# Sigmoid of twelve gate tiles taken where they are computed, two y tiles kept on chip, and 35 small transfers begun by ScalarE

## The chip, the cores and the metric

The kernel runs on one core of a Trainium2 chip. The metric is device time in microseconds, from the first to the last instruction of one execution with what lies around it. A core has five engines that run side by side, each with its own instruction queue, worked through in order: TensorE (PE in the profile, with its weight loads as PEld), VectorE (DVE), ScalarE (ACT), GpSimd (POOL) and SyncE (SP). A DMA is begun by an instruction in one of these queues; before the change all are begun from SP's.

## The reference

One layer of a hybrid trunk on 1024 rows of 1024 channels, float32. One projection yields queries, keys and values for two branches of eight heads, and the two gates:

```python
h = x @ w_in[l]
qa, ka, va, qb, kb, vb, ga, gb = jnp.split(h, split_pts, axis=-1)
y_a = chunk_band_attention(...qa, ka, va, rel_bias[l]) @ w_proj_a[l]   # softmax over a band
y_b = stick_breaking_attention(...qb, kb, vb) @ w_proj_b[l]            # sigmoids, cumulative products
gate_a = jax.nn.sigmoid(ga + b_gate[l, :D])
gate_b = jax.nn.sigmoid(gb + b_gate[l, D:])
mix = (gate_a * y_a + gate_b * y_b) @ w_out[l]
x = layer_norm(DEEPNORM_ALPHA * x + mix, ln1_g[l], ln1_b[l])
...                                                                   # SwiGLU block, second layer norm
```

## The kernel before

Each large product is made from numbers split into a high and a low part (`split`: ScalarE casts the high part, VectorE or GpSimd subtracts), so three matmuls stand for one. Tiles of 128 partitions by 1024 columns come from pools of slots by tag (`SLOTS`): a new tile takes the slot of the one allocated so many allocations before with the same tag, and waits until that one is done with. The order of the instructions on each engine is set at build time from the order in which the program states them, with an estimate of what is ready when; at run time each engine keeps that order.

**First stage, the projections** (to about 367 us). 18 pairs of column blocks. One is computed plainly, the others with seven half-size products in place of eight (`pair_steps`, L176; matmuls at L173). The last six pairs are gates: pair j gives 128 channels of branch A's gate and the same 128 of branch B's, for j below `N_GATE` = 6. The halves of a result tile are put together by ScalarE's copies (L190, L199, L203, and L372 for the last one) and VectorE's additions (L186). `out_g` (L365) then stores the raw gate tile to `g_dr` from SP's queue. The tiles of this stage live in the slots in which the attention's queries, keys and values arrive later (tags qs, kh, kl, v), so the first of those loads wait for the last stores.

**Attention** (367 to about 676 us). Branch A's eight heads come first, then branch B's. A head has 12 value steps: a step transposes weights on TensorE (L575), splits them (`pt`, L111 and L112) and multiplies with the values (L588, L589). Scores for later steps run ahead (L478, L479). In branch A VectorE adds the bias (L509), ScalarE takes exponentials (L514) and GpSimd scales (L517). In branch B ScalarE takes two sigmoids (`kp` L542, `w` L543), VectorE a cumulative product (L546, L550), and GpSimd a product (L552). At the end of each half of a head ScalarE copies the 128-row result out of its bank (L603), and a transfer on chip of 64 rows by 512 columns (L604, 128 KB) brings the second half of the products to the partitions of the first. Three steps later GpSimd adds them into the pair's tile `yt` (L607). After the last of four additions `yt` is stored to `y_dr[i]` (L609). That is done for pairs 0 to 6; pair 7 is cut where it lies. There are 31 such small transfers, 16 of them in branch A.

**Fill.** Between the value steps TensorE is given other matmuls (`fill_all`, L616): first the remaining four gate tiles (pairs 6 and 7 of each branch, `gate`, L422, stored at L437), then branch A's output projection over eight channel blocks c (matmuls L675). For it `fetch_y` (L620) loads `y_dr[i]` back into `yraw`, and `cut_y` (L624) splits it into yh (ScalarE, L627) and yl (GpSimd, L628). For each c, `fetch_g` loads the gate tile gA, `sigma` (L699) takes its sigmoid in place on ScalarE (L701), queued half a block ahead, and VectorE multiplies the projection with it (L678). Blocks 0 to 4 are stored to `m_dr`, 5 to 7 are kept. The fill runs at 8 matmuls a head in branch A and at 40 in branch B.

**Merge** (676 to about 715 us). For c in the order 6, 7, 5, 4, 0, 1, 2, 3 the gate gB of branch B is loaded (L793), its sigmoid taken (L794), the projection of branch B multiplied with it (L805), branch A's part added (L806), and the sum split for the output projection. After that come the output projection, the layer norm and the SwiGLU block, which the change does not touch.

Of the kernel before, what the change touches and what calls it, by code (L numbers as in the profile page):

```python
# [49 lines left out]
def hybrid_trunk_kernel(ctx: ExitStack, tc, x, xt, w_in, b_gate, rel_bias, w_proj,  # L50
# [14 lines left out]
    def slot(tag, name, dtype=F32):  # L65
        return pool.tile([P, 1024], dtype, tag=tag, name=name, bufs=SLOTS[tag])
# [236 lines left out]
    def project_plain(i):  # L303
# [20 lines left out]
                store_hl(d[pair], h, t)  # L324
        return take

    def project(i):
        kind, pair = work[i][:2]
        tl = {}

        def tile_of(side):
            if side not in tl:
                tl[side] = cycle(QKV, f"c{side}_{i}")
            return tl[side]

        def c(name):
            return tile_of(name[1])[:, (LO, HI)[int(name[0]) - 1]]

        def out_qk(side):
            scale = (-0.125 if pair < 4 else 0.125) if side == "1" else 1.0  # L340
            t = tl[side]
            h = cycle(QKV, f"hi{side}_{i}", F32R)
            nc.scalar.activation(h, t, AF.Copy, scale=scale)
            nc.vector.scalar_tensor_tensor(t, t, scale, h.bitcast(F32), ALU.mult, ALU.subtract)
            d = (q_dr, k_dr)[side == "2"]
            store_hl(d[pair], h, t)

        def out_v(side):
            pr = pair + int(side) - 1
            vs = [cycle(QKV, f"v{pr}_{h}", F32R).rearrange("p (t c) -> p t c", t=8)  # L350
                  for h in range(2)]
            for hf in range(2):
                tp = bank("tr", f"vtp{pr}_{hf}")
                for j in range(4):
                    o = hf * HW + j * P
                    tr(tp[:, j * P:(j + 1) * P], tl[side][:, o:o + P], ident)
                t3 = tp.rearrange("p (t c) -> p t c", t=4)
                ts_ = slice(4 * hf, 4 * hf + 4)
                for h in range(2):
                    split(vs[h][:, ts_, 0:DH], vs[h][:, ts_, DH:P],  # L360
                          t3[:, :, h * DH:(h + 1) * DH])
            for h in range(2):
                dma(v_dr[2 * pr + h].rearrange("p (t c) -> p t c", t=8), vs[h].bitcast(F32))

        def out_g(side):  # L365
            dma(g_dr[2 * pair + int(side) - 1], tl[side])

        out = dict(qk=out_qk, v=out_v, g=out_g)[kind]

        def done(name, acc):  # L370
            if name == "21":
                nc.scalar.copy(c("21"), acc)  # L372
                out("1")
            elif name == "12":
                out("2")

        return pair_steps(f"p{i}", Wa[i], ops_x, c, done)
# [44 lines left out]
    def gate(i, w, half=lambda: None, then=lambda k: None):  # L422
        gt = slot("gt", f"gate{i}")
        for hf, cs in enumerate((LO, HI)):
            acc = bank("mm", f"gps{i}_{hf}")
            for k in range(KT):
                ks = slice(k * P, (k + 1) * P)
                for j, (lw, rx) in enumerate(((w[0], xh), (w[0], xl), (w[1], xh))):
                    mm(acc, lw[:, ks], rx[k][:, cs], start=(k == j == 0),  # L429
                       stop=(k == KT - 1 and j == 2))  # L430
                    yield 1.0
                if hf == 1:
                    then(k)
            nc.scalar.copy(gt[:, cs], acc)
            if hf == 0:
                half()
        dma(g_dr[i], gt)  # L437

    left(2)
    take = project_plain(0)  # L440
# [115 lines left out]
    def value_steps(hd, g, wt):  # L556

        br, h = hd["br"], hd["h"]
        reach = (4, 8)[br]
        q0 = 4 * g  # L560
        nm = f"{'ab'[br]}{hd['n']}_{g}"
        pv = []

        kbs = [4, 5, 6, 7, 3, 2, 1, 0] if g == 0 else [7, 6, 5, 4]
        steps = []
        for i, kb in enumerate(kbs):
            lo_q = max(q0, kb - reach)
            hi_q = min(q0 + 3, kb)
            n = (hi_q - lo_q + 1) * P
            pts = []  # L570

            def turn(kb=kb, lo_q=lo_q, hi_q=hi_q, n=n, pts=pts):
                tp = bank("tr", f"tp_{nm}_{kb}")
                for qb in range(lo_q, hi_q + 1):
                    tr(tp[:, (qb - lo_q) * P:(qb - lo_q + 1) * P],  # L575
                       wt[qb - q0][:, (kb - qb) * P:(kb - qb + 1) * P], ident)
                pt = slot("pt", f"pt_{nm}_{kb}", F32R)
                split(pt[:, 0:n], pt[:, HW:HW + n], tp[:, 0:n])
                pts.append(pt)

            def mult(i=i, kb=kb, lo_q=lo_q, n=n, pts=pts):
                v = hd["v"]
                if i == 0:
                    pv.append(bank("pv", f"pv_{nm}"))
                last = i == len(kbs) - 1
                cs = slice((lo_q - q0) * P, (lo_q - q0) * P + n)
                pt = pts[0]
                mm(pv[0][:, cs], v[:, kb, :], pt[:, 0:n], start=(i == 0), stop=False)  # L588
                mm(pv[0][:, cs], v[:, kb, :], pt[:, HW:HW + n], start=False, stop=last)  # L589
                if last:  # L590
                    yt = hd["yt"]()
                    r = slice(h * DH, (h + 1) * DH)
                    gs = slice(g * HW, (g + 1) * HW)
                    if hd["i"] == 7 and h == g == 1:
                        nc.scalar.copy(yt[r, gs], pv[0][DH:P])
                        nc.vector.tensor_tensor(yt[r, gs], pv[0][0:DH], yt[r, gs], ALU.add)
                    else:

                        if g == 0:
                            hd["yv"] = slot("yt", f"yv_{nm}")  # L600
                        yv = hd["yv"]
                        both, other = (yt, yv) if h == 0 else (yv, yt)
                        nc.scalar.copy(both[:, gs], pv[0])  # L603
                        dma(other[r, gs], both[(DH, 0)[h]:(P, DH)[h], gs])  # L604

                        def add():
                            nc.gpsimd.tensor_tensor(yt[r, gs], yt[r, gs], yv[r, gs], ALU.add)  # L607
                            if h == 1 and g == 1:
                                dma(y_dr[hd["i"]], yt)  # L609
                        later.append([3, add])  # L610

            steps.append((turn, mult))
        return steps


    def fill_all():  # L616
# [5 lines left out]
            dma(yraw[i], y_dr[i])  # L622

        def cut_y(i):  # L624
            yh[i] = slot("xt", f"yh{i}", F32R)
            yl[i] = slot("xt", f"yl{i}", F32R)
            nc.scalar.copy(yh[i], yraw[i])  # L627
            nc.gpsimd.tensor_tensor(yl[i], yraw[i], yh[i].bitcast(F32), ALU.subtract)  # L628

        def fetch_g(c):  # L630
            gA[c] = slot("gt", f"gA{c}")
# [17 lines left out]
        for i in range(first_gate, 16):  # L649
# [3 lines left out]
            else:  # L653
# [1 line left out]
                fetch_y(0)  # L655
                fetch_y(1)
                yield from gate(i, w[-1], lambda: half_of(i), then)
        sigma(gA[0], 0, 0)
        for cc in range(4):
            wh, wl = w[-1]  # L660
            if cc < 3:
                nxt = fetch_proj(0, cc + 1, "op")
            if cc:
                fetch_y(3 + cc)
            for j in range(2):
                c = 2 * cc + j
                t = gA[c]
                if c < 7:
                    fetch_g(c + 1)
                for hf, cs in enumerate((LO, HI)):  # L670
                    acc = bank("mm", f"yAps{c}_{hf}")
                    for k in range(4):
                        ks = slice(j * HW + k * P, j * HW + (k + 1) * P)
                        for n, (lw, rx) in enumerate(((wh, yh), (wh, yl), (wl, yh))):
                            mm(acc, lw[:, ks], rx[k][:, cs], start=(k == n == 0),  # L675
                               stop=(k == 3 and n == 2))
                            yield 1.0
                    nc.vector.tensor_tensor(t[:, cs], acc, t[:, cs], ALU.mult)  # L678
                    if hf == 0 and c < 7:
                        sigma(gA[c + 1], c + 1, 0)  # L680
                if c < KEEP:
                    dma(m_dr[c], t)
                else:
                    kept[c] = t
                if j == 0 and cc < 3:
                    w.append(cut_w(nxt, f"y0_{cc + 1}", of("op"), nc.gpsimd))
                if j == 0 and cc:
                    cut_y(3 + cc)

    def fetch_proj(br, cc, raw):  # L690

# [4 lines left out]
    KEEP, kept = 5, {}  # L696
    yh, yl = [None] * 8, [None] * 8

    def sigma(t, c, br):  # L699
        col = br * 8 + c  # L700
        nc.scalar.activation(t, t, AF.Sigmoid, bias=bg[:, col:col + 1])  # L701

    fill = fill_all()
    state = dict(t=0.0, done=False)
# [84 lines left out]
    for n, c in enumerate((6, 7, 5, 4, 0, 1, 2, 3)):  # L789
# [1 line left out]
            w = cut_w(fetch_proj(1, c // 2, "op"), f"y1_{c // 2}", of("op"), nc.vector)  # L791
        gB = slot("kp", f"gB{c}")
        dma(gB, g_dr[2 * c + 1])  # L793
        sigma(gB, c, 1)  # L794
        if c in kept:
            mA = kept[c]
        else:
# [370 lines left out]
```

## Time and profile before

| | |
|---|---|
| median of 3 runs | 1471.09 us (1469.01 to 1471.99) |
| the profiled execution | 1470.15 us |
| its span, first to last instruction | 1468.4 us |
| busy: PE, DVE, ACT, POOL | 1430.9, 1038.5, 675.3, 277.8 us |
| mean granted TensorE clock | 0.997 |

The profile names an instruction by its line, its engine and the tiles it writes and reads (`gA<-gA,bg`). A row of a timeline gives start, duration, and in brackets the idle time of the engine before it with what ended that. "The chain of work" is followed back from the last instruction: at each step to what released it. The granted clock is TensorE's, 1.00 at full speed.

### The profile page before, as it was taken

What the parts mean: (1) busy time and instruction counts of PE and PEld (TensorE: products, weight loads), DVE (VectorE), ACT (ScalarE), POOL (GpSimd) and SP (SyncE); (2) the same over time, 40 slices, a digit from 0 to 9 for tenths busy, and PEclk for the clock granted to TensorE, in tenths of its full rate; (3) what the DMA queues carried; (4) which work ended last, traced back from release to release, by engine and by line L of the source; (5) the groups of instructions that cost most, each with busy time, mean ns of one, the idle gap of its engine ahead of it and who ended that gap; (6) DMA issues with size and microseconds to landing.
All of it is one profiled execution on the core that took longest, in us unless ns stands there. A gap on an engine that the chain in (4) does not pass through costs nothing.

```text
span 1468.4 us, 19171 instructions
## 1 busy us (share of the span) xinstructions
PE 1430.9 (97%) x6728; PEld 1179.3 (80%) x6728; DVE 1038.5 (71%) x1702; ACT 675.3 (46%) x1180; POOL 277.8 (19%) x327
## 2 busy tenths in 40 slices
PE   8999999999999999899999999999999999999997
PEld 6788888888788788777888888888888887888886
DVE  8866655442787987786948966767777665978767
ACT  6444444332888878774513534444444433221201
POOL 0000000000566779761004100000000000100016
PEclk9999999999999999999999999999999999999999
DMA  6555545326777567648711123444444456786602
GB/s 215 158 188 173 161 144 180 121 83 212 193 234 215 156 177 231 196 145 287 236 42 72 56 89 129 158 158 148 154 146 154 144 201 241 291 310 234 213 15 100
DMA packets 83696, 248.12 MB, mean 169 GB/s; under 512 B 10560, under 2 KB 10560, under 8 KB 83600
## 3 DMA queue, kind: packets, MB, share of 16 engines
q1 hardware_dynamic: 83600, 246.90, 51.1%
q8 instruction: 53, 0.87, 0.2%
q14 instruction: 43, 0.35, 0.1%
HBM read 162.03 MB, written 80.77 MB: 165 GB/s over the span
## 4 chain that ended last, share of the span: by engine, by line
PE 82%; DVE 7%; DMA 5%; ACT 2%; issue 2%; SPq 1%; POOL 0%; POOLq 0%; DVEq 0%; ACTq 0%
PE sxf L173 15%; PE sxp L173 12%; PE szf L173 7%; PE szp L173 6%; PE dx L1101 6%; PE syf L173 4%; PE dz L1101 3%; PE syp L173 3%; PE gps L429 2%; DVE kp_b L550 2%; PE ops L121 2%; PE ops L119 2%; PE ops L118 2%; PE fpswh_h L118 1%; PE fpswh_h L121 1%
## 5 line engine op out<-in xcount | busy, mean ns | idle before, releaser
L1057 POOL TENSOR_TENSOR wdyt<-wdyt 128x512 f32<-128x512 f32 x8 | 10.7, 1335 | 515.9 <-DVE wdgt L1056 491.2
L552 POOL TENSOR_TENSOR w_b<-w_b,kp_b 128x511 f32<-128x511 f32 (+3 forms) x96 | 97.0, 1021 | 32.3 <-DVE kp_b L550 21.7
L550 DVE TENSOR_TENSOR_SCAN kp_b<-kp_b,ident_ps 128x384 f32<-128x384 f32 (+6 forms) x88 | 78.5, 892 | 4.8
L186 DVE TENSOR_TENSOR c<-sxp,c 128x512 f32<-128x512 f32 x17 | 11.8, 692 | 79.3 <-issue 46.1
L496 POOL MEMSET bias<- 64x64 f32 x8 | 1.2, 144 | 349.5 <-ACT bias L495 349.4
L821 POOL TENSOR_TENSOR mv<-mv,neghalf 128x1 f32<-128x1 f32 x16 | 23.8, 1485 | 195.9 <-DVE mv L820 195.9
L542 ACT ACTIVATE kp_b<-sc_b 128x512 f32<-128x512 f32 (+3 forms) x96 | 49.0, 510 | 22.5 <-PE sc_b L479 21.1
L112 DVE TENSOR_TENSOR pt_b<-tp_b,pt_b 128x512 fp32r<-128x512 f32 (+1 forms) x96 | 49.8, 541 | 9.5 <-ACT pt_b L111 9.4
L173 PE MATMUL szf<-x1S63h,wcf 128*128 128x512 f32 x168 | 55.1, 389 | 0.0
L1032 DVE TENSOR_TENSOR x<-dx,x 128x512 f32<-128x512 f32 x64 | 43.3, 687 | 15.5 <-PE dx L1101 15.5
L575 PE MATMUL tp_b<-ident,w_b 128*128 128x128 f32 x288 | 48.8, 279 | 5.0 <-DVE pt_b L112 4.4
L112 DVE TENSOR_TENSOR sl<-h,sl 128x512 fp32r<-128x512 f32 x56 | 38.4, 686 | 20.2 <-ACT sl L111 20.2
L111 ACT CAST sl<-h 128x512 fp32r<-128x512 f32 x56 | 34.7, 619 | 36.1 <-PE syf L173 17.1
L118 PE MATMUL ops<-wh_o,mh 128*128 128x512 f32 x128 | 50.2, 392 | 0.0
L121 PE MATMUL ops<-wh_o,ml 128*128 128x512 f32 x128 | 50.0, 391 | 0.0
L111 ACT CAST pt_b<-tp_b 128x512 fp32r<-128x512 f32 (+1 forms) x96 | 47.2, 510 | 6.0 <-PE tp_b L575 5.4
L119 PE MATMUL ops<-wl_o,mh 128*128 128x512 f32 x128 | 49.9, 390 | 0.0
L517 POOL TENSOR_SCALAR w_a<-w_a,st_a 128x640 f32<-128x640 f32 (+2 forms) x64 | 42.4, 668 | 36.8 <-DVE st_a L516 23.4
L543 ACT ACTIVATE w_b<-sc_b 128x511 f32<-128x511 f32 (+3 forms) x96 | 49.1, 512 | 0.0
L575 PEld LDWEIGHTS tp_b<-ident,w_b 128*128 128x128 f32 x288 | 35.1, 142 | 17.3 <-DVE pt_b L112 8.4
L112 DVE TENSOR_TENSOR pt_a<-tp_a,pt_a 128x512 fp32r<-128x512 f32 (+1 forms) x96 | 44.5, 485 | 4.8 <-ACT pt_a L111 3.8
L111 ACT CAST pt_a<-tp_a 128x512 fp32r<-128x512 f32 (+1 forms) x96 | 39.6, 428 | 16.1 <-PE tp_a L575 15.6
(1923 smaller groups left out, 4805.4 us busy)
## 6 DMA issues: line engine op xcount, KB each, us to landing
s_dr<-sl SPq DMA_DIRECT2D x112, 256.0 KB, 2.3
sd<-s_dr SPq DMA_DIRECT2D x56, 512.0 KB, 4.5
wLf<-in_w_ffn_in_dram SPq DMA_DIRECT2D x22, 512.0 KB, 4.2
wRf<-in_w_ffn_in_dram SPq DMA_DIRECT2D x22, 512.0 KB, 3.6
wLp<-in_w_in_dram SPq DMA_DIRECT2D x18, 512.0 KB, 5.1
wRp<-in_w_in_dram SPq DMA_DIRECT2D x18, 512.0 KB, 4.1
v_dr<-v SPq DMA_DIRECT2D x16, 512.0 KB, 4.0
kl<-k_dr SPq DMA_DIRECT2D x32, 256.0 KB, 5.8
```

The costliest lines, as they stand in the source:

```text
L111: nc.scalar.copy(dst_h, src)
L112: nc.vector.tensor_tensor(dst_l, src, dst_h.bitcast(F32), ALU.subtract)
L118: mm(acc, lh, rh, start=(i == 0), stop=False)
L119: mm(acc, lh, rl, start=False, stop=False)
L121: mm(acc, ll, rh, start=False, stop=(i == n))
L173: mm(acc, lw[:, ks], rx, start=(first and kt == i == 0), stop=(kt == 3 and i == 2), skip_group_check=not first)
L542: nc.scalar.activation(kp[:, c0:e], sc[:, 0:n], AF.Sigmoid, scale=-1.0)
L543: nc.scalar.activation(be[:, m0:e], sc[:, m0 - c0:n], AF.Sigmoid)
L550: nc.vector.tensor_tensor_scan(kp[:, s0:e], kp[:, s0:e], ident_ps()[:, 0:e - s0], kp[:, s0 - 1:s0], ALU.mult, ALU.bypass)
L552: nc.gpsimd.tensor_tensor(be[:, m0:e], be[:, m0:e], kp[:, m0 - 1:e - 1], ALU.mult)
L575: tr(tp[:, (qb - lo_q) * P:(qb - lo_q + 1) * P], wt[qb - q0][:, (kb - qb) * P:(kb - qb + 1) * P], ident)
L1101: mm(acc, a, b, start=(first and i == n == 0), stop=(i == n - 1 == 1), skip_group_check=not first)
```

## The change

1. `out_g` takes the sigmoid of the tile, with its bias, before storing it. The twelve gate tiles of the seven-product pairs are thus stored finished. `sigma` is left out in the fill for c below 6 and in the merge for c below 6; c = 6 and 7 keep it.
2. When y of pairs 5 and 6 is complete, `keep_y` cuts it at once from `yt`; it is not stored and not loaded back. Pairs 0 to 4 go through `y_dr` as before. Two tiles `yraw` fewer are taken from the tag "op", so that later tiles of that tag fall on other slots.
3. The 31 small transfers and the four gate stores of `gate` are begun from ScalarE's queue, each right behind ScalarE's own copy.

```diff
+    def sigma(t, c, br):
+        col = br * 8 + c
+        nc.scalar.activation(t, t, AF.Sigmoid, bias=bg[:, col:col + 1])
...
         def out_g(side):
+            sigma(tl[side], pair, int(side) - 1)
             dma(g_dr[2 * pair + int(side) - 1], tl[side])
...
-        dma(g_dr[i], gt)
+        nc.scalar.dma_start(g_dr[i], gt)
...
                         nc.scalar.copy(both[:, gs], pv[0])
-                        dma(other[r, gs], both[(DH, 0)[h]:(P, DH)[h], gs])
+                        nc.scalar.dma_start(other[r, gs], both[(DH, 0)[h]:(P, DH)[h], gs])
 
                         def add():
                             nc.gpsimd.tensor_tensor(yt[r, gs], yt[r, gs], yv[r, gs], ALU.add)
                             if h == 1 and g == 1:
-                                dma(y_dr[hd["i"]], yt)
+                                if hd["i"] < 5:
+                                    dma(y_dr[hd["i"]], yt)
+                                else:
+                                    keep_y(hd["i"], yt)
...
         def cut_y(i):
-            yh[i] = slot("xt", f"yh{i}", F32R)
-            yl[i] = slot("xt", f"yl{i}", F32R)
-            nc.scalar.copy(yh[i], yraw[i])
-            nc.gpsimd.tensor_tensor(yl[i], yraw[i], yh[i].bitcast(F32), ALU.subtract)
+            keep_y(i, yraw[i])
...
-        sigma(gA[0], 0, 0)
...
-            if cc:
-                fetch_y(3 + cc)
+            if cc == 1:
+                fetch_y(4)
...
-                    if hf == 0 and c < 7:
+                    if hf == 0 and N_GATE <= c + 1 < 8:
                         sigma(gA[c + 1], c + 1, 0)
...
-                if j == 0 and cc:
-                    cut_y(3 + cc)
+                if j == 0 and cc == 1:
+                    cut_y(4)
...
+    def keep_y(i, raw):
+        yh[i] = slot("xt", f"yh{i}", F32R)
+        yl[i] = slot("xt", f"yl{i}", F32R)
+        nc.scalar.copy(yh[i], raw)
+        nc.gpsimd.tensor_tensor(yl[i], raw, yh[i].bitcast(F32), ALU.subtract)
...
         dma(gB, g_dr[2 * c + 1])
-        sigma(gB, c, 1)
+        if c >= N_GATE:
+            sigma(gB, c, 1)
```

More of the change, by code (lines that the diff above doesn't have):

```diff
@@ L697, in hybrid_trunk_kernel @@
     yh, yl = [None] * 8, [None] * 8
-    def sigma(t, c, br):
-        col = br * 8 + c
-        nc.scalar.activation(t, t, AF.Sigmoid, bias=bg[:, col:col + 1])
+    def keep_y(i, raw):
[3 more added lines that the diff above has]
+        nc.gpsimd.tensor_tensor(yl[i], raw, yh[i].bitcast(F32), ALU.subtract)
     fill = fill_all()
```

## The prediction

> **What bounds the kernel now.** I read the page first, then a table by stages, then the two worst stages and the two stage borders as timelines and as the chain of work.
>
> ```profile
> span 1468.4 us, 19171 instructions
> ...
> PE 1430.9 (97%) x6728; PEld 1179.3 (80%) x6728; DVE 1038.5 (71%) x1702; ACT 675.3 (46%) x1180; POOL 277.8 (19%) x327
> ```
>
> PE is busy for all but 37.5 us, so a gain must come from PE's idle time or from its clock. The stages, as windows (start:end, length, then busy time of PE, PEld, DVE, ACT, POOL, then the granted clock and the share of the DMA engines):
>
> ```profile
> 0.00:367.00 367.00, 357.35 (x1589) 292.95 (x1590) 212.91 (x282) 154.68 (x217) 3.81 (x14) 1.00 0.51 163
> 367.00:381.00 14.00, 11.90 (x67) 9.40 (x66) 8.47 (x37) 9.96 (x24) 8.05 (x12) 1.00 0.88 200
> 381.00:490.00 109.00, 103.92 (x650) 87.82 (x649) 94.31 (x330) 93.52 (x245) 67.51 (x98) 1.00 0.72 207
> 490.00:585.00 95.00, 93.27 (x524) 78.17 (x523) 80.02 (x137) 79.10 (x179) 79.91 (x99) 1.00 0.65 194
> 585.00:600.00 15.00, 10.73 (x42) 8.01 (x42) 8.14 (x12) 7.52 (x15) 9.03 (x13) 0.77 0.71 212
> 648.00:655.00 7.00, 4.58 (x26) 3.06 (x25) 3.51 (x8) 5.71 (x12) 4.63 (x4) 1.00 0.28 106
> 676.00:715.00 39.00, 37.85 (x165) 29.87 (x164) 31.97 (x45) 18.07 (x24) 1.29 (x1) 1.00 0.89 294
> ```
>
> Projections (to 367) run on PE alone. Branch A (381 to 490) loses 109.00 - 103.92 = 5.1 us with DVE and ACT both at 86% of the time: no single bound. Branch B has two holes: 585 to 600 (15.00 - 10.73 = 4.27 us idle, and a granted clock of 0.77) and 648 to 655 (7.00 - 4.58 = 2.42 us idle). The merge (676 to 715) loses 1.15 us. The change touches all of these places.
>
> **The change part by part.**
>
> *First hole (the six early sigmoids of branch A's gates leave the fill).* ScalarE's timeline, then TensorE's and GpSimd's; the bracket is the idle time before an instruction and what ended it:
>
> ```profile
> 582.69 0.59 ACT L603 COPY yv_b<-pv_b 128x512 f32<-128x512 f32 x1
> 587.81 1.15 ACT L701 ACTIVATE gA<-gA,bg 128x1024 f32<-128x1024 f32 x1 [4.53 <-DMA gA<-g_dr]
> 588.87 0.58 ACT L542 ACTIVATE kp_b<-sc_b 128x512 f32<-128x512 f32 x1
> ...
> 589.99 0.44 PE L478 MATMUL sc_b<-kh,qs 128*128 128x384 f32 x1 [2.72 <-ACT w_b L543]
> ...
> 592.97 1.11 PE L575 MATMUL tp_b<-ident,w_b 128*128 128x128 f32 x4 [1.19 <-DVE pt_b L112]
> ...
> 591.09 2.66 POOL L552 TENSOR_TENSOR w_b<-w_b,kp_b 128x511 f32<-128x511 f32 x2 [3.43 <-DVE kp_b L550]
> 593.84 1.27 POOL L607 TENSOR_TENSOR yt<-yt,yv_b 64x512 f32<-64x512 f32 x1
> ```
>
> One in-place sigmoid on a gate tile stands in ScalarE's queue waiting 4.53 us for its load; behind it stands kp_b, which empties the score bank, and TensorE stands for that. In the timeline it is the fourth of the eight on branch A's gates, so channel block 3, which the change takes: below block 6 the gate arrives finished, and its only reader is DVE's product (L678) half a block later. TensorE gets back 4.27 us of idle and the half-speed stretch after it, 15.00 x (1 - 0.77) = 3.45 us: 7.7 together. What is late next is GpSimd: it was idle 3.43 us, less than TensorE's 4.27, so about 0.8 of the gain meets its queue; I take another 0.4 for loads that still land late. Gain 6.5; bounds 0 (the wait returns elsewhere, below) and 7.7.
>
> *Second hole (y5 and y6 cut from the tile that GpSimd finished, not from DRAM).* The chain of work and the two engines:
>
> ```profile
> 643.03 2.84 DMA y_dr<-yt
> 645.89 4.37 DMA yraw<-y_dr
> ...
> 650.29 1.05 ACT L627 CAST yh<-yraw 128x1024 fp32r<-128x1024 f32 x1 [1.29 <-DMA yraw<-y_dr]
> ...
> 652.05 0.50 PE L478 MATMUL sc_b<-kh,qs 128*128 128x512 f32 x1 [0.80 <-ACT w_b L543]
> ...
> 654.40 0.44 PE L575 MATMUL tp_b<-ident,w_b 128*128 128x128 f32 x2 [1.61 <-DVE pt_b L112]
> ```
>
> The store and load of y6 take 2.84 + 4.37 = 7.2 us, ScalarE waits 1.29 for them, and TensorE 0.80 + 1.61 = 2.41. With y6 kept, the cast and GpSimd's subtraction are the same instructions, earlier, at about 643. Gain 2.4; bounds 0 and 2.4. The new wait: the cast now stands in ScalarE's queue behind GpSimd's add (L607), which itself waits for a small transfer. For y6 the add ended before 643.03, so nothing is late. For y5 it ended at 593.84 + 1.27 = 595.1, and what would queue behind the cast is again kp_b; that is a rival.
>
> *Branch B, the rest.* The small transfers and the gate stores move from SP's queue to ScalarE's. Price of one issue, from SP's own, and what the landing took; then what SP waited for at that line, and the group of sigmoids:
>
> ```profile
> L604 SPq DMA_DIRECT2D yv_a<-yt x8: 477/477/491, 387.7 to 473.8; - x8
> ...
> DMA to landing us min/median/max: 2.2/3.1/8.3
> ...
> SPq L604 <- ACT pt_a L111: 25.9, 5, 9.4
> ...
> L701 ACT ACTIVATE gA<-gA,bg 128x1024 f32<-128x1024 f32 x8 | 9.5, 1184 | 7.6 <-DMA gA<-g_dr 7.6
> ...
> L437 SPq DMA_DIRECT2D g_dr<-gate x4: 325/348/580, 458.6 to 564.1; - x4
> ```
>
> 35 issues (31 small transfers, 4 stores) at about 0.48 us are 16.8 us of ScalarE's sequencer. Each waits only for ScalarE's own copy just before it, so the wait is short and the 0.48 is the cost; what stands behind it are exponentials, kp_b and the casts of pt. 18 fall in branch B: 8.6 us, against six sigmoids gone, 6 x 1.18 = 7.1. Net 1.5 us of ScalarE work in a stage where it is busy 79.10 of 95.00; I take a third on the path, +0.5; bounds -7.1 and +8.6.
>
> *Branch A.* 17 issues, 8.2 us, and nothing removed: ScalarE goes from 93.52 to 101.7 busy of 109.00. How much of that TensorE sees stands between ScalarE's share of the chain (the first line, 6.5% for w_a and 4.8% for pt_a) and its share of the time. Against it, SP no longer stands at that line (25.9 us in the largest group above) with loads behind it, and two transfers lie on this stage's chain:
>
> ```profile
> by line: PE tp_a L575 15.7%; PE sc_a L478 10.4%; PE pv_a L588 10.2%; PE pv_a L589 9.6%; PE sc_a L479 8.4%; DVE kp_b L550 7.2%; ACT w_a L514 6.5%; PE gps L429 4.8%; ACT pt_a L111 4.8%; issue 4.7%; DMA kh<-k_dr 3.5%; DVE pt_a L112 3.3%; DMA y
> ...
> 432.09 2.45 DMA yt<-yv_a
> ...
> 436.31 3.81 DMA kh<-k_dr
> ```
>
> Bounds -6.3 (both transfers hidden, 2.45 + 3.81) and +8.2; I take a quarter of 8.2, +2.0, nearer to the chain's share than to the busy share.
>
> *First stage and its border.* Twelve sigmoids of 1.18 us are added. Eleven lie in a stage where ScalarE is busy 154.68 of 367.00 and are hidden in its idle time (12 to 13 us if that cover were gone). The stores behind them leave 1.2 us later, and with them the weight loads queued on SP behind a store; TensorE idles only 9.7 us in this stage, so I take 0. The twelfth is not hidden. The border's chain, ScalarE's rows there, and the table loads:
>
> ```profile
> 367.12 0.60 ACT c L372
> ...
> 367.74 2.90 DMA g_dr<-c
> ...
> 371.02 9.03 DMA kh<-k_dr
> ...
> 380.19 0.39 PE sc_a L478
> ...
> 367.61 1.05 ACT L409 CAST wh_g<-wr_g 128x1024 fp32r<-128x1024 f32 x1
> 368.77 0.83 ACT L514 ACTIVATE w_a<-w_a,st_a 128x640 f32<-128x640 f32 x1
> ...
> L111 ACT ACT_TABLE_LOAD x1 | 1.3, 1283 | 0.7 <-PEq L1158 0.7
> L542 ACT ACT_TABLE_LOAD x1 | 1.3, 1283 | 0.0
> ```
>
> The last gate tile's copy, its store, and the key load that reuses its slot end TensorE's longest idle time of this border (380.19). The sigmoid enters between copy and store: +1.2, or +2.2 if the wh_g cast (1.05) is queued ahead of it. On ScalarE the exponentials start later by 1.2 plus one more table load (1.28), because sigmoids now precede the first exponential: 2.4. The two delays run side by side; bounds +1.2 and +2.4, I take +1.8.
>
> The Trainium skill, "ScalarE: Activation LUTs", section "What ACT_TABLE_LOAD costs", prices a switch of tables at about 2.66 us, the load and a drain of 1.38, and its rules for authors ask to group calls by table set, which speaks against this step. By that the border would cost 1.4 more, an estimate; the rows here show 1.28 and no drain.
>
> *Merge.* Six more sigmoids go, of the same form and length; DVE's product now waits for the gate's load itself. TensorE lost only 1.15 there: gain 0.6, bounds 0 and 1.15.
>
> Sum: -6.5 - 2.4 + 0.5 + 2.0 + 1.8 - 0.6 = -5.2. The profiled execution took 1470.15 us, 0.94 below the median of the runs, 1471.09; 1470.15 - 5.2 = 1465.0.
>
> **The rivals.**
>
> *A larger gain:* freed of its waits, SP issues branch A's loads so early that both transfers leave the chain: -6.3 in place of +2.0, 1456.7. For it: SP's waits; against: the DMA engines are already 72% busy there. 0.12.
>
> *The wait comes back:* the cast of y5 stands behind GpSimd's add. That small transfer is the slow one (8.3 us is the maximum above), and GpSimd adds only after two w_b products. If ScalarE reaches the cast at about 585 it stands as long as before, and 6.5 is lost: 1471.5. Against: the transfer no longer queues behind SP's loads. 0.16.
>
> *Slower:* ScalarE becomes the bound of the two attention stages, and all 16.8 us of issues are on the path, in place of my 2.5: 1465.0 + 14.3 = 1479.3. It decides from 63% on the path (2.5 + 8.1 of 16.8). For it: 86% busy in branch A; against: its small share of the chain. 0.14.
>
> *The border cools the clock:* 2.1 us of TensorE idle there (14.00 - 11.90) grows by up to 2.4 to 4.5, more than the 4.27 that ended in a clock of 0.77, while the 2.42 us did not (1.00). Then 3.45 more: 1468.4. 0.08. [...]
>
> **How the numbers follow.** My case: 0.50, 1465, its own range 1460 to 1468. About 0.2% (2.9 us) is what a measurement can tell. Faster: my case and the larger gain, 0.62. The returned wait and the cold border fall within 0.2%: 0.24. Slower: 0.14. The range reaches from the larger gain to beyond the returned wait, with part of branch A's upper bound: 1456 to 1475.
>
> **What would show it.** The sigmoid line with 4 executions in the fill and 12 in the first stage; no wait for a gate load near 585, and a granted clock of 1.00 there; y loads five in place of seven; a table load more, at the first exponential; ScalarE's idle time before the two casts of kept y small. Wrong, if branch A grows by over 4 us, if ScalarE waits for GpSimd's add, or if a new hole opens between 580 and 650.

## The result, and the profile after

The changed kernel takes 1480.36 us (median of 6 runs, 1476.95 to 1484.15), the kernel before 1469.22 us over 6 runs (1467.40 to 1471.99): a ratio of 1.0077, 95% interval 1.0057 to 1.0096. The change costs 11 us; the prediction was a gain of 5, with 1456 to 1475 us as its range. The profiled execution spans 10.5 us more than that of before. The head of its page:

```profile
span 1478.9 us, 19115 instructions
...
PE 1435.2 (97%) x6728; PEld 1183.4 (80%) x6728; DVE 1036.8 (70%) x1702; ACT 681.3 (46%) x1182; POOL 275.8 (19%) x327
...
q10 hardware_dynamic: 3056, 6.16, 1.5%
```

TensorE executes the same 6728 instructions, but its busy time grows by 4.3 us: some of them ran at a lower clock. The rest of the 10.5 us is idle time. The last line is new: ScalarE's own DMA queue (packets, MB, share of the 16 DMA engines' span), with the 35 transfers that the change gave it.

The same windows as before, cut at about the same points of the work (columns: start:end, length, busy time of PE, PEld, DVE, ACT, POOL, granted clock, DMA share, GB/s):

```profile
367.00:381.00 14.00, 13.72 (x75) 10.62 (x73) 9.03 (x38) 13.02 (x29) 8.21 (x13) 1.00 0.92 275
381.00:500.50 119.50, 108.68 (x651) 91.65 (x651) 92.91 (x329) 94.36 (x247) 66.37 (x97) 0.97 0.68 184
500.50:597.00 96.50, 92.72 (x515) 77.37 (x514) 79.63 (x138) 76.44 (x175) 79.95 (x102) 0.98 0.64 199
597.00:612.00 15.00, 9.71 (x43) 7.08 (x42) 8.13 (x12) 8.64 (x17) 9.31 (x10) 0.87 0.48 134
612.00:662.00 50.00, 47.34 (x253) 38.82 (x253) 42.23 (x71) 36.77 (x83) 35.98 (x45) 0.97 0.51 158
688.00:727.00 39.00, 38.18 (x172) 31.38 (x171) 33.60 (x48) 15.19 (x21) 1.28 (x1) 1.00 0.90 309
```

Branch A, 109.00 us before, takes 119.50: nearly the whole loss (9.6 us by where the first head behind it begins, below; the windows' ends differ by a few matmuls). Of its 10.5 us, 5.7 are TensorE idle (119.50 - 108.68 = 10.82 against 5.08) and 4.8 are a longer busy time. Of these, 3.4 are two stretches of 3.4 us at half speed, shown below; the rest is not accounted for. ScalarE is busy 94.36 us in a longer stage, against 93.52. Its 17 issues, 8.0 us by their rows, are not counted in that, but during 5.9 of the 8.0 us it executes other instructions, so some 96 of 119.50 us are taken: it is no bound. Branch B up to the hole takes 96.50 for 95.00; the hole is still there, 12 us later, with 5.29 us idle instead of 4.27; behind it the rest takes 50.00 for 48.00. The merge loses 0.82 instead of 1.15.

Where a head begins its products with the values, the two traces stand apart by (after minus before, us; worked out from the matmul records; "merge" is the first matmul of branch B's projection, "FFN" that of the SwiGLU block):

```
head       0     1     2     3     4     5      6      7     8     9    10    11     12     13     14     15   merge  FFN  end
         +1.8   0.0  +3.8  +5.3  +6.2  +8.2  +11.6  +10.3  +9.6  +8.1  +8.2  +8.2  +11.9  +13.1  +14.5  +12.8  +12.5 +11.1 +10.5
```

**How branch A loses it.** One head of it, all engines' timelines; first before, where ScalarE empties the value bank (L603), SyncE begins the small transfer (L604), loads for the next head (values L471, queries L460, keys L463), and GpSimd adds the halves (L607):

```profile
390.81 0.33 SPq L471 DMA_DIRECT2D v<-v_dr  x1
...
391.23 0.38 SPq L460 DMA_DIRECT2D qs<-q_dr  x1
...
392.32 0.60 ACT L603 COPY yt<-pv_a 128x512 f32<-128x512 f32 x1
...
392.94 0.49 SPq L604 DMA_DIRECT2D yv_a<-yt  x1
...
393.48 1.24 SPq L463 DMA_DIRECT2D kh<-k_dr  x2
...
394.76 1.23 SPq L463 DMA_DIRECT2D kl<-k_dr  x2
...
396.52 1.29 POOL L607 TENSOR_TENSOR yt<-yt,yv_a 64x512 f32<-64x512 f32 x1
```

and the same place after (the lines are now L608, L609, L468 for the keys and L612):

```profile
390.62 0.44 SPq L468 DMA_DIRECT2D kh<-k_dr  x1
...
391.15 0.54 SPq L476 DMA_DIRECT2D v<-v_dr  x1
...
391.74 0.42 SPq L465 DMA_DIRECT2D qs<-q_dr  x1
391.75 0.59 ACT L608 COPY yt<-pv_a 128x512 f32<-128x512 f32 x1
...
392.21 0.45 SPq L468 DMA_DIRECT2D kh<-k_dr  x1
392.37 0.47 ACTq L609 DMA_DIRECT2D yv_a<-yt  x1
...
392.71 1.24 SPq L468 DMA_DIRECT2D kl<-k_dr  x2
...
401.32 1.29 POOL L612 TENSOR_TENSOR yt<-yt,yv_a 64x512 f32<-64x512 f32 x1 [5.19 <-DMA yv_a<-yt]
...
402.60 0.80 POOL L522 TENSOR_SCALAR w_a<-w_a,st_a 128x640 f32<-128x640 f32 x1
...
403.45 0.33 PE L580 MATMUL tp_a<-ident,w_a 128*128 128x128 f32 x1 [0.72 <-POOL w_a L522]
...
403.78 2.24 POOL L522 TENSOR_SCALAR w_a<-w_a,st_a 128x640 f32<-128x640 f32 x3
...
404.64 0.33 PE L580 MATMUL tp_a<-ident,w_a 128*128 128x128 f32 x1 [0.85 <-POOL w_a L522]
```

Before, the loads of values and queries had been begun 2.1 and 1.7 us ahead of the small transfer. Then SyncE stood for the copy, began the small transfer 0.02 us after it (its end: 392.32 + 0.60), and all four key loads came after that. The transfer had a start on them, and the add began 3.6 us after the copy. After, the transfer begins just as soon behind the copy, 0.03 us: there was no issue delay to save. But SyncE, freed, has begun two of the key loads ahead of it, one 0.16 us before, with values and queries less than 1.3 us before, and it begins the other two right behind. The 128 KB share the DMA engines with them: by the DMA records their packets move only from 396.0 to 400.3 us, 3.6 us and more after the issue. The add begins 9.0 us after the copy, with 5.19 us of GpSimd standing for the transfer. The softmax scaling of w_a (L522) is queued behind the add, and TensorE's transposes stand for it 0.72 and 0.85 us. Over the whole kernel, at the line of the small transfers:

```profile
L609 ACTq DMA_DIRECT2D yv_a<-yt x8: 468/479/512, 387.6 to 484.5; - x8
...
  POOL yt L612: 53.0, 15
...
DMA to landing us min/median/max: 2.2/4.4/8.9
```

Before, the landing had a median of 3.1 us and GpSimd's wait was 15.8 us over 7 times (the same view at L604); after, 4.4 and 53.0 us over 15. Branch A's 16 transfers alone, by their records, took 2.99 us from issue to landing in the mean before and 5.79 after; below, "branch A's landing" is this mean in the profiled execution of a run. TensorE's two largest waits in branch A after, and the largest before:

```profile
PE tp_a L580 <- POOL w_a L522: 4.3, 7, 0.9
PE sc_a L484 <- DMA kl<-k_dr: 2.8, 2, 2.0
```

```profile
PE tp_a L575 <- DVE pt_a L112: 1.9, 4, 0.8
```

The listed waits on w_a are short (0.9 us at most), but idle time close together was followed by half speed. The windows around the head above:

```profile
402.00:404.00 2.00, 1.06 (x6) 0.57 (x4) 1.20 (x7) 1.18 (x5) 1.85 (x5) 1.00 0.35 88
404.00:406.00 2.00, 0.92 (x6) 0.73 (x7) 0.00 (x0) 0.22 (x1) 2.00 (x3) 1.00 0.00 0
406.00:408.00 2.00, 2.00 (x12) 1.96 (x11) 1.67 (x8) 1.50 (x5) 1.41 (x3) 0.66 0.43 127
408.00:410.00 2.00, 2.00 (x9) 1.84 (x8) 1.37 (x5) 1.73 (x6) 1.33 (x3) 0.50 1.09 328
```

GpSimd is full in the first two (1.85 and 2.00 of 2.00), TensorE half idle in gaps of at most 0.9 us, and then it runs 3.4 us at half speed. A second stretch of 3.4 us begins near 454, behind gaps of 0.85 and 2.0 us; before there was none in branch A. In the whole kernel such stretches add up to 17.1 us, against 6.8 before, leaving out one at the very end of both; where TensorE is busy throughout, each costs half its length. The Trainium skill, "TensorE: Matmul & The Clock Gate", section "Why this matters for your kernels", ties the lower clock to idle gaps over some 3 us; these two places had none so long.

### The profile page after: what moved, and what is told of

The parts are those of the page before. It is cut to its first block, busy times and chain, and to the rows that moved or that the text cites. A ratio compares the mean times of both kernels' runs of the same rounds, so it can differ in the third digit from the quotient of the medians.

```text
span 1478.9 us, 19115 instructions
## 1 busy us (share of the span) xinstructions
PE 1435.2 (97%) x6728; PEld 1183.4 (80%) x6728; DVE 1036.8 (70%) x1702; ACT 681.3 (46%) x1182; POOL 275.8 (19%) x327
## 4 chain that ended last, share of the span: by engine, by line
PE 59%; DVE 4%; DMA 3%; POOL 1%; issue 1%; ACT 1%; SPq 0%; POOLq 0%; ACTq 0%; DVEq 0%
PE sxf L173 15%; PE szf L173 7%; PE dx L1108 6%; PE syf L173 4%; PE dz L1108 3%; PE gps L434 2%; PE yAps L679 2%; PE ops L121 2%; PE ops L119 2%; PE ops L118 2%; PE tp_b L580 2%; PE fpswh_h L118 1%; PE dy L1108 1%; PE fpswh_h L119 1%; PE fpswh_h L121 1%; DVE kp_b L555 1%
## 5 line engine op out<-in xcount | busy, mean ns | idle before, releaser
L580 PE MATMUL tp_a<-ident,w_a 128*128 128x128 f32 x240 | 46.7, 283 | 6.3 <-POOL w_a L522 4.6
L111 ACT CAST sl<-h 128x512 fp32r<-128x512 f32 x56 | 34.7, 619 | 35.7 <-PE syf L173 17.1
L519 ACT ACTIVATE w_a<-w_a,st_a 128x640 f32<-128x640 f32 (+2 forms) x64 | 44.7, 699 | 11.9 <-DVE st_a L514 9.2
L522 POOL TENSOR_SCALAR w_a<-w_a,st_a 128x640 f32<-128x640 f32 (+2 forms) x64 | 42.1, 666 | 28.7 <-DVE st_a L521 26.3
```

Source lines behind the costliest of these rows:

```text
L111: nc.scalar.copy(dst_h, src)
L580: tr(tp[:, (qb - lo_q) * P:(qb - lo_q + 1) * P], wt[qb - q0][:, (kb - qb) * P:(kb - qb + 1) * P], ident)
```

## The experiments

All ratios are to the kernel before, run on the same chip beside each; its median there was 1469.86 us for the first four experiments, 1469.51 for the next four and 1469.41 for the last two. The L numbers in rows are those of the run's own kernel.

### Small transfers back on SyncE

```diff
-  nc.scalar.dma_start(other[r, gs], both[(DH, 0)[h]:(P, DH)[h], gs])
+  dma(other[r, gs], both[(DH, 0)[h]:(P, DH)[h], gs])
```

> The changed kernel with the 31 small transfers begun from SP's queue again; gate stores, sigmoids and kept y as changed. If the transfers' queue is the cause, by their landing or by their issue, the loss goes and the gains of the rest appear: 1458 to 1467 us, and GpSimd's waits for small transfers fall from 53 us to below 20. If the sigmoids or the kept y are the cause: 1476 to 1484.

1473.37 us, ratio 1.0020 (1.0008 to 1.0032), 3.5 us above the kernel before, where the changed kernel was 11.1 above it. Over seven of the eleven us come back with this one line, but not the forecast gain. Branch A's landing is 3.34 us, against 5.79 in the changed kernel and 2.99 before; GpSimd's waits for small transfers fall from 53.0 to 22.5 us.

One thing besides the queue differs. The build puts the instructions in another order when the small transfers change queue: of GpSimd's 280 instructions from 365 to 720 us, 240 stand in the same sequence in this kernel and in the changed one. This experiment and the next therefore don't tell the queue from the order; the fifth does.

### Only the small transfers on ScalarE, on the kernel before

The same line changed the other way in the kernel before; sigmoids, y and gate stores stay as they were.

> The kernel before with nothing changed but the 31 small transfers begun from ScalarE's queue. Landing theory (the loads behind them on SP start at the same time, the transfer lands later, GpSimd's add stands in its queue): branch A grows by 8 to 12 us, the mean time from issue to landing there goes from 3.0 to over 5 us, and the total is 1479 to 1487. Issue theory: the same total, but GpSimd does not wait more. If the sigmoids or the kept y are the cause: 1467 to 1472.

1487.07 us, ratio 1.0119 (1.0100 to 1.0139). The one line alone, with the order that the build gives it (239 of GpSimd's 280 in the same sequence), makes the kernel 17 us slower: sigmoids and kept y are not needed for the loss. Branch A's landing is 5.12 us, and TensorE's wait on w_a, which the list of branch A's waits before doesn't show, is there:

```profile
PE tp_a L575 <- POOL w_a L517: 4.4, 7, 1.4
```

### The issue without the transfer

To tell ScalarE's issue time from the landing: small transfers on SyncE, and behind each copy ScalarE begins a transfer of 64 x 4 bytes to DRAM that nobody reads.

```diff
   dma(other[r, gs], both[(DH, 0)[h]:(P, DH)[h], gs])
...
+  nc.scalar.dma_start(junk_dr[jn][0:DH, 0:1],
+                      both[(DH, 0)[h]:(P, DH)[h], gs.start:gs.start + 1])
```

> As e1_small_sp, and ScalarE begins a transfer of 64 rows of 4 bytes to DRAM right behind each of the 31 copies, which nothing waits for: the price of the issue alone. Landing theory: within 2 us of e1_small_sp. Issue theory: 8 us or more above it.

1477.52 us, ratio 1.0058 (1.0040 to 1.0075): 4.1 us more than the same kernel without the dummies, between the two forecasts (under 2, and 8 or more). The true transfers land later too (branch A's landing is 4.37 us against 3.34), and the order is again another one (253 of GpSimd's 280), so 4.1 us is not the price of 31 issues; and the two profiled executions, 1474.6 and 1474.5 us, don't show it. That ScalarE pays all of its 31 x 0.47 = 14.6 us of issues does not fit this result.

### A later add

```diff
-  later.append([3, add])
+  later.append([6, add])
```

> The changed kernel, with GpSimd's additions stated six value steps behind the transfer in place of three. The issue on ScalarE and the landing stay as they are. Landing theory: GpSimd waits less than 25 us for the small transfers in place of 53, branch A shrinks by 5 to 11 us, total 1465 to 1474. Issue theory: no change, 1478 to 1483.

1480.59 us, ratio 1.0074 (1.0050 to 1.0098). It tells nothing: the instructions were put in practically the same order as in the changed kernel, so GpSimd came to the add as early as there, and its waits are of the same size. That a later add would hide the landing stays open.

### SyncE made to stand for the copy again

The changed kernel whole, with ScalarE still beginning the small transfers. One thing is added: SyncE, too, begins a transfer of 64 x 4 bytes from the copied tile, and so waits for the copy as it did before.

```diff
   nc.scalar.dma_start(other[r, gs], both[(DH, 0)[h]:(P, DH)[h], gs])
...
+  dma(junk_dr[jn][0:DH, 0:1], both[(DH, 0)[h]:(P, DH)[h], gs.start:gs.start + 1])
```

> The changed kernel, small transfers still begun by ScalarE, and at each of the 31 places SP also begins a transfer of 64 rows of 4 bytes from the same copied tile to DRAM. So SP stands for the copy as before the change, and the loads queued behind start after the small transfer, not beside it. Landing theory: mean time from issue to landing in branch A falls from 5.8 us to below 4.5, GpSimd's waits there from 32 us to below 18, the total by 3 to 9 us (1471 to 1477). If the loads' start plays no part: 1478 to 1484, landing unchanged.

1468.57 us, ratio 0.9989 (0.9980 to 0.9999): 0.9 us under the kernel before, where the changed kernel was 11.1 above it, though this one does more; the forecast of 1471 to 1477 was too modest. The order of the instructions is that of the changed kernel (all 280 of GpSimd's in the same sequence), so the order isn't the cause, nor is ScalarE's issuing: what is new is that SyncE stands, and its next loads come later. At the place shown above GpSimd comes to the same add as early as there and waits 0.25 us instead of 5.19. The transfer, issued at 392.23, has its packets moved from 394.6 to 395.2 us:

```profile
396.24 1.29 POOL L616 TENSOR_TENSOR yt<-yt,yv_a 64x512 f32<-64x512 f32 x1 [0.25 <-DMA yv_a<-yt]
```

Branch A's landing falls from 5.79 to 4.48 us, and GpSimd's idle time before the 16 adds there from 31.9 to 15.5 us. Over all runs, the landing is 2.73 to 3.34 us in the seven kernels in which SyncE begins the transfers, 5.12 to 5.79 in the three in which ScalarE does, and 4.37 and 4.48 in the two with dummies. If the dummies cost 1.03 us of landing here too, as the third experiment suggests (4.37 - 3.34), 3.45 remain, about what the transfers took from SyncE's queue (3.34); then ScalarE's queue itself would not be what is slow. The Trainium skill, "DMA: Bandwidth & Descriptors", section "Issuing engines are not separate DMA queues", says that transfers begun by different engines share the same 16 DMA engines and interleave, and that more issuing engines save only issue time. The traces agree: 0.03 us from copy to issue in both kernels (0.02 to 0.07 at all but four of the 31 transfers before and all but two after), and a landing of 5.79 for 2.99 us.

### Sigmoids and kept y, all transfers begun by SyncE

The changed kernel with both DMA lines as before: its first two parts alone.

> Parts 1 and 2 of the change alone: all transfers begun from SP. Landing theory for the gate stores too: SP's wait of 8.9 us at a gate load, for the store of the slot's former tile, falls below 2, and ScalarE's wait of 5.4 us for a weight load of branch A's projection below 2: 1464 to 1471, 3 us or more below e1_small_sp. ScalarE still waits for GpSimd's add before the casts of kept y, 3 to 7 us. If the gate stores' queue plays no part: as e1_small_sp, 1472 to 1476.

1469.27 us, ratio 1.0000 (0.9988 to 1.0012). Against the first experiment only the four gate stores differ, begun by ScalarE there and by SyncE here: they cost 3.8 us by the medians against the kernel before (1.0020 and 1.0000, whose intervals overlap a little). How, in the first experiment's rows (SyncE's and ScalarE's issues, and who stands):

```profile
563.15 0.33 ACTq L442 DMA_DIRECT2D g_dr<-gate  x1
...
572.10 0.33 SPq L637 DMA_DIRECT2D gA<-g_dr  x1
572.52 0.85 SPq L408 DMA_DIRECT2D wr_y<-in_w_proj_dram  x2
...
578.74 1.04 ACT L414 CAST wh_y<-wr_y 128x1024 fp32r<-128x1024 f32 x1 [5.44 <-DMA wr_y<-in_w_proj_dram]
...
580.71 0.79 PE L593 MATMUL pv_b<-pt_b,v 128*128 128x512 f32 x1 [4.93 <-ACT yv_b L608]
```

The store lands 8.9 us after its issue, among loads that SyncE has begun (4.7 at most with SyncE issuing it). SyncE stands 8.9 us for it (1.8 with SyncE issuing it) at the gate load that reuses the slot, the weight load behind it leaves late, ScalarE stands 5.44 us for the weights, and TensorE 4.93. The changed kernel has the same chain, with shorter waits of ScalarE and TensorE (below). So has the experiment above, with 4.03 and 4.06 us, and its time is 1468.57 us all the same: the price of the stores depends on what else is late.

### The sigmoids alone

As the last, and y5 and y6 go through DRAM as before.

> Part 1 of the change alone: sigmoids in the first stage, y through DRAM, all transfers begun from SP. If the casts of kept y are a cause in branch B: 1460 to 1467, 3 us or more below e6_sigma_keep, the hole near 585 gone and the one near 650 left. If keeping y helps as predicted: 2 us or more above e6_sigma_keep.

1465.24 us, ratio 0.9973 (0.9958 to 0.9989): the only part that gains, 4 us, and a version faster than both kernels. The hole near 585 is not gone, though, as had been expected: it lies near 604, with another load (below). Keeping the two y takes these 4 us away again (1469.27).

### The cast of the kept y moved to GpSimd

```diff
-  nc.scalar.copy(yh[i], raw)
+  if i < 5: nc.scalar.copy(yh[i], raw)
+  else: nc.gpsimd.tensor_copy(yh[i], raw)
```

on the kernel with sigmoids and kept y.

> As e6_sigma_keep, with the high part of the two kept y taken by GpSimd itself, behind its own add, so that ScalarE no longer stands for it; GpSimd gets two more casts of a 128x1024 tile, 1 to 2.5 us each. If ScalarE's wait for the add is what costs: 1459 to 1466, below e6_sigma_keep by 2 us or more. If not: no lower.

1469.49 us, ratio 1.0001 (0.9991 to 1.0011): no gain, where 1459 to 1466 had been expected. ScalarE no longer stands for GpSimd's add, but for the next thing in its queue:

```profile
605.81 1.04 ACT L414 CAST wh_y<-wr_y 128x1024 fp32r<-128x1024 f32 x1 [8.84 <-DMA wr_y<-in_w_proj_dram]
```

### Casts of loads taken later, without and with the kept y

In the kernel with the sigmoids alone, and in the one with sigmoids and kept y, the casts of weights and of loaded y come half a channel block later in the program. The edit in short, not word for word:

```diff
-  if j == 0: cut next weights; cut_y          # after the even block
+  if hf == 0 and j == 1: cut next weights; cut_y   # after half of the odd block
```

> The kernel with the early sigmoids alone (1465.2 us, all transfers begun by SyncE), with one more edit: in the fill of branch B the casts of the next projection weights and of the loaded y stand half a channel block later in ScalarE's queue (after the first half of the odd block, not after the whole even block); nothing is left out. Theory (the hole near 590 to 605 is ScalarE standing in its queue for a load that lands late in a stretch where the DMA engines are full): the 5.66 us wait for yraw before the cast of y falls below 2 us, TensorE's 3.93 us of idle and its half-speed stretch go, 1461.5 to 1463.5 us. Rival (the same stretch of loads makes the next thing late, the queries and keys of the next head or GpSimd's add, whatever ScalarE waits for): a hole of 3 us or more stays between 590 and 615 with another releaser, 1464.5 to 1466.5 us.

1465.80 us, ratio 0.9970 (0.9958 to 0.9982): as without the edit. The wait stays, and its row shows why it could not help: SyncE issues the load of y5 only at 599.53.

```profile
583.86 0.66 SPq L468 DMA_DIRECT2D kh<-k_dr  x1
593.26 0.32 SPq L614 DMA_DIRECT2D y_dr<-yt  x1
...
599.11 0.33 SPq L634 DMA_DIRECT2D gA<-g_dr  x1
599.53 0.38 SPq L627 DMA_DIRECT2D yraw<-y_dr  x1
```

```profile
591.95 1.28 POOL L612 TENSOR_TENSOR yt<-yt,yv_b 64x512 f32<-64x512 f32 x1 [2.11 <-DMA yt<-yv_b]
```

```profile
604.52 1.04 ACT L704 CAST yh<-yraw 128x1024 fp32r<-128x1024 f32 x1 [5.64 <-DMA yraw<-y_dr]
```

SyncE stands 9 us, from 584.5 to 593.3, for GpSimd's add of y5 so as to store it, and the add stands for its small transfer. A store of `m_dr` behind it leaves late too; SyncE stands 2.6 us for that store at the gate load of 599.11, and only then comes to y5. The theory that ScalarE merely asked too early fell: the load was issued late.

> The kernel with the early sigmoids and the two y kept on chip (1469.3 us, all transfers begun by SyncE), with the same edit: the casts of the next projection weights and of the loaded y stand half a channel block later; the casts of the two kept y stay directly behind GpSimd's add. Nothing is left out. Theory (the y that is kept costs 4 us because its cast waits behind GpSimd's add and so makes a hole that the load did not make): the edit doesn't touch that wait, the 6.95 us before yh<-yt near 592 stays above 4 us, 1468 to 1470 us. Rival (the kept y is only one of several late things, and the casts of weights and loads set the hole as much): the wait falls to under 3 us or its hole is made up later, 1463 to 1466 us.

1469.81 us, ratio 1.0005 (0.9995 to 1.0015): as without the edit, and the wait is where the theory left it.

```profile
590.41 1.26 POOL L612 TENSOR_TENSOR yt<-yt,yv_b 64x512 f32<-64x512 f32 x1 [4.36 <-DMA yt<-yv_b]
...
591.71 1.04 ACT L707 CAST yh<-yt 128x1024 fp32r<-128x1024 f32 x1 [7.50 <-POOL yt L612]
```

Both runs lead back to the same transfer, `yt<-yv_b` of y5's last half; TensorE idles 4.70 us here. Through DRAM its lateness reaches ScalarE by way of SyncE, the store and the load; kept on chip, directly.

## Why the prediction was wrong

By medians, each run against the kernel before on its own chip, the parts add up so, in this order: sigmoids alone -4.3, kept y +4.0, gate stores on ScalarE +3.8, small transfers on ScalarE +7.6; together +11.1. The sequence matters: the small transfers alone on the kernel before cost 17. What the prediction named as signs of being wrong all came: branch A grew by over 4 us, ScalarE waited for GpSimd's add, and a hole opened between 580 and 650. Its terms one by one:

- **Branch A, +2.0 predicted, +10.5 measured. This is the step that failed most, and by its mechanism.** I priced ScalarE's issues, and counted SyncE's 25.9 us at the line as waits whose removal could only help. An issue takes ScalarE's queue what I took (0.47 us, against 0.48), but I counted it as busy time of the engine, and it mostly isn't: ScalarE executes other instructions during 5.9 of the 8.0 us that branch A's 17 issues take, 9.3 of 16.1 in the whole kernel. The stage is not longer by ScalarE's work. SyncE's wait held its loads back behind the small transfer, and taking it away let them compete with it. GpSimd's adds, with w_a behind them, then stood for the transfers. The same error carried the rival of a larger gain: SyncE's loads did start earlier, and that was the loss. The prediction's "slower" case forecast 1479.3 us and the time came out near, but by chance, for a reason that it did not contain: making SyncE stand again took the time from 11.1 us above the kernel before to 0.9 below it, with every issue still on ScalarE.
- **First hole, -6.5 predicted; not removed.** The gate load's wait did go, as predicted: there is no sigmoid of a gate in the fill near 585, and 4 are left of 16.

```profile
L329 ACT ACTIVATE c<-c,bg 128x1024 f32<-128x1024 f32 x12 | 13.8, 1153 | 6.2 <-DVE c L186 5.7
```

 But the step "what is late next" charged 0.8 + 0.4 us for it, and it was the whole wait. In the changed kernel ScalarE stands for weights and then for the add of y5:

```profile
585.83 1.04 ACT L414 CAST wh_y<-wr_y 128x1024 fp32r<-128x1024 f32 x1 [2.83 <-DMA wr_y<-in_w_proj_dram]
...
587.42 0.70 PE L593 MATMUL pv_b<-pt_b,v 128*128 128x512 f32 x1 [2.86 <-ACT yv_b L608]
...
603.91 1.26 POOL L612 TENSOR_TENSOR yt<-yt,yv_b 64x512 f32<-64x512 f32 x1 [4.57 <-DMA yt<-yv_b]
605.20 1.04 ACT L706 CAST yh<-yt 128x1024 fp32r<-128x1024 f32 x1 [6.36 <-POOL yt L612]
...
607.07 0.42 PE L483 MATMUL sc_b<-kh,qs 128*128 128x320 f32 x1 [3.60 <-ACT w_b L548]
```

 Heads 11 to 13, from the first value products of one to those of the next, take 76.0 us before, 82.4 after, 73.9 with the sigmoids alone. Even there 2.2 us are gained, not 6.5: the load of y5 takes the gate load's place.
- **Kept y: the rival "the wait comes back" came true** (6.36 us, forecast "as long as before"), and it is what cancels the sigmoids' gain in the version without the DMA moves. My argument against it, that the transfer no longer queues behind SyncE's loads, failed on its premise: y5's last transfer landed 8.27 us after its issue from SyncE's queue before and 8.54 from ScalarE's after, and 8.42 with kept y and all transfers on SyncE. Its queue made no difference. Before, GpSimd came to the add at 593.84, when the transfer had landed (583.31 + 8.27 = 591.58); after, it comes sooner after the issue and stands 4.57 us.
- **Second hole, -2.4 predicted.** The size came out about right: the head before the last, in which it lay, takes 22.68 us for 24.42, -1.7, and no y load ends a wait there. That kept y did it is not shown. With kept y and all transfers on SyncE that head takes 25.00 us, with 2.88 us of TensorE idle in place of 2.42, and ScalarE stands 3.65 us for GpSimd's add of y6, of which I had said that nothing is late; with the small transfers alone moved, and y through DRAM, it takes 22.93.
- **Border, +1.8 predicted.** Head 0's value products begin 1.8 us later, as predicted; head 1 stands at 0.0. The exponentials' late start (371.22 for 368.77; two table loads more, not the one forecast) costs nothing in the end, a give-back that the term lacked. The border did not cool the clock: 1.00, with 14.00 - 13.72 = 0.28 us of TensorE idle. That rival had taken the first hole's 4.27 us for one gap; by TensorE's records they are gaps of 2.72, 0.35 and 1.19 us.
- **Merge, -0.6 predicted, -1.4 measured** (44.51 us for 45.88, first to last matmul of branch B's projection).
- **The gate stores,** three issues inside the term of +0.5 and one inside branch A's, cost 3.8 us in the version without the other move. The issue is 0.33 us; the price is their landing (there 6.5 us at the median for 4.1) at a slot that SyncE waits for.

Open: whether a later add would cover the landing (the one trial left the order as it was), and what would shorten the transfer of y5's last half in branch B, from which the hole follows in the changed kernel and in the two versions of the last experiments (where SyncE was made to stand, it landed in 4.49 us; why, I have not followed up). ScalarE's pure issue cost is not measured by itself; with all 35 issues on ScalarE and SyncE standing, the time was 1468.57 us, against 1469.27 with all on SyncE. Heads 11 to 13 also shift between versions in ways that I have not followed up.

## What to carry to other kernels

A wait in an in-order DMA queue can be a priority: what stands behind the waiting issue doesn't compete with the transfer that is waited for. Before moving a small transfer on which an engine depends to another queue, list the loads that its wait holds back, and price the landing beside them rather than the issue. When a wait goes from a stretch in which several things are late, ask what each later instruction of the same engine's queue needs, and when that was issued; a hole that is only passed on brings nothing.

## What the runs showed of the hardware that I had not expected

- The same 128 KB transfer, begun 0.03 us behind its producer in both kernels, landed in branch A in 2.99 us (mean) where the key loads were issued behind it and in 5.79 where some of them were issued ahead of it and the others at the same time from another engine's queue.
- ScalarE executes other instructions while its queue issues a DMA: during 9.3 of the 16.1 us that the changed kernel's 35 issues take.
- With 31 dummy transfers of 256 bytes each, branch A's landing was 4.37 us in place of 3.34 and, by the medians of the runs, the time 4.1 us longer. The order of the instructions differed in part, so it is not shown that the dummies alone did it; but it speaks against taking a transfer for free because it is small.
- A half-speed stretch of 3.4 us followed a cluster of TensorE gaps of at most 0.9 us each, half idle over 4 us, while 2.42 us of idle in 7 us before (gaps of 0.80 and 1.61) had left the clock at 1.00.
